# Stores of the residual and of finished gated blocks issued by GpSimd instead of ScalarE

## The chip, the cores and the metric

The kernel runs on one core of a Trainium2 chip. The metric is the device time of one execution in microseconds. Each time given for a kernel is the median of several runs. The profile comes from one more execution, recorded by the hardware profiler. In it PE is TensorE's matmuls, PEld its weight loads, DVE is VectorE, ACT is ScalarE, POOL is GpSimd and SP is SyncE. SP does no arithmetic here: it only issues transfers. A name with a q behind it (ACTq) is that engine's sequencer, which waits for semaphores and issues transfers while the engine itself works on.

## The reference, cut to what matters

One layer of an encoder over 1024 positions of width 1024, in float32. Two attentions share one input projection and one output projection; then comes a gated feed-forward block of width 2816. The part in which the change lies:

```python
h = h + jnp.einsum('bsd,df->bsf', mix, w_out)          # the residual h1
hn = rmsnorm(h, norm_ffn)
g = jnp.einsum('bsd,df->bsf', hn, w_gate)              # 1024 -> 2816
u = jnp.einsum('bsd,df->bsf', hn, w_up)
g = conv_width_3_over_positions(g) + conv_b
h = h + jnp.einsum('bsf,fd->bsd', silu(g) * u, w_down) # 2816 -> 1024
out = rmsnorm(h, norm_final)
```

## The kernel before

Everything is kept transposed: 128 features on the partitions, the 1024 positions along the free dimension, in two halves of 512. A float32 operand is split into a high and a low half, and each block product is three matmuls (high by high, high by low, low by high; function `group`, lines 986 to 988). The halves of the weights come from `split_w`: ACT copies the high half (line 960), DVE subtracts (line 961). In the attention the same is done at lines 169 and 170.

The stages in order of time, in the profiled execution: input projection and attention up to about 376 us, the output projection up to about 420 us, the gated block up to about 820 us, the down projection up to about 1016 us, and a tail in which the last columns are normed and stored.

**Output projection** (loop at line 1049). For each half h and each of 8 feature tiles d, PE makes a bank, and `settle_out` (line 1003) finishes the one before: DVE adds the residual input (line 1006), the sum h1 is stored to DRAM (`spilled`, line 1007), ACT squares it (line 1009) and DVE adds the squares up (line 1011). These are 16 stores of 256 KB. The sums in SBUF are later scaled in place for the norm (`normed`, line 1016) and turned into operands (`operand`, line 993), while the copies in DRAM are read back at the end (`residual`, line 1388) to be added to the down projection.

**Gated block** (class `Gated`). The products follow a scheme of seven instead of eight block products (names 11, 12, s1, s2, s4, s3, 22), so that sums and differences of operands and weights are made on DVE (`sub`, line 1025; lines 1095 to 1108). Each of 22 units makes gate and up for 128 features. `p1` and `p5` copy banks with ACT (`copy_bank`, line 1027), `p2`, `p3` and `p7` add with DVE (`join`, line 1026), `conv` does the convolution and SiLU (lines 1160 to 1163), and `p4` multiplies (lines 1170, 1171). Its result u, the finished gated block, is stored by `keep` (line 1188) to a tile `x` in DRAM. The first 11 units and the last 11 are paired; `sums` (line 1194) makes three differences of a pair (tiles t23 and t4) and stores them with `keep` too. That is 22 stores of a whole unit's block (512 KB), 11 of t23 (512 KB) and 11 of t4 (256 KB). For the first four units the store is put off: `to_keep` holds it, and the main loop does two at a time under `behind("joined")`, which queues it after the ACT evacuation marked "joined" (line 1151) on that evacuation's engine.

**Down projection** (loop at line 1452). It reads the stored blocks back (`x_load`, line 1303, issued by SP), splits them (`x_split`: ACT line 1309, DVE line 1310) and multiplies them with w_down, whose halves SP loads (`down_raw`, line 1277) four groups ahead. `x_load`, `down_raw` for all but the last product and `residual` keep their order on SP's queue. The feature tiles 2 and 5 are finished by POOL (line 1424), the others by DVE.

**What sets the order.** PE's order is the order of the program (it is scheduled by hand). The other engines' queues are laid out by a planner when the kernel is built. It goes by priorities and modelled times of all instructions, issues of transfers among them, and it assigns buffers too: tiles of one tag share a number of buffers (`op` 14, `mix` 8, `tt` 6), and a tile that takes a buffer over waits until the last reader of the former tile is done, a store included. Each queue then runs strictly in order. Before the change ACT issues the 60 stores, SP issues all loads, and POOL issues no transfer at all.

Of the kernel before, what the change touches and what calls it, by code (L numbers as in the profile page):

```python
# [56 lines left out]
def hybrid_layer(tc, xT, w_first, w_in, w_out, w_gate, w_up, w_down, small, sink, rpb, consts, rope, out):  # L57
    nc = tc.nc
    with ExitStack() as ctx:
# [13 lines left out]
        def big(name, tag, dt=F32):  # L73
            return lpool.tile([128, S], dt, name=name, tag=tag, bufs=slots[tag])
# [8 lines left out]
        tsl = lambda h: slice(h * HALF, (h + 1) * HALF)  # L83
# [20 lines left out]
        for name, dst, n in (("h", his, 2), ("h", his, 2), ("l", los, 2), ("l", los, 2), ("w", None, 2)):  # L104
            t = flat(big(name, "mix", F32R)[:, :], n)
# [581 lines left out]
        t = quarters(big("f", "mix"))  # L687
# [137 lines left out]
        for g in range(2):  # L825
            for b in range(NB):
                q, t = unit_window(g, b)
# [53 lines left out]
        for u in range(len(flat)):  # L881
            q, t, need, kind = flat[u]
# [69 lines left out]
        spilled = [dram.tile([128, S], F32, name="h1d", tag=f"h1d{d}") for d in range(KT)]  # L952
# [48 lines left out]
        at = lambda k, h: h1[k][:, tsl(h)]  # L1001

        def settle_out():
            d, h, ps = late.pop(0)
            with tc.high_priority(offset=500):
                nc.vector.tensor_tensor(sv(at(d, h)), pv(ps[:, :]), sv(at(d, h)), op=ALU.add)
            nc.scalar.dma_start(spilled[d][:, tsl(h)], at(d, h))
            s2 = half("s2")
            nc.scalar.activation(s2, at(d, h), AF.Square)
            if total[h] is not None:  # L1010
                nc.vector.tensor_tensor(s2, s2, total[h], op=ALU.add)
            total[h] = s2
# [36 lines left out]
        for h in range(2):  # L1049
            for d in range(KT):  # L1050
                if h == 0 and d + 2 < KT:
                    wo.append(load_wo(d + 2, fpool))
                ps = bank("pj", ("o", "s", "pj")[(h * KT + d) % 3])
                for _ in product(ps, wo[d], mg[4:8], h):
                    pass
                late.append((d, h, ps))
                if h == 1 and d == 1:
                    v = inverse_narrow([total[0]], D, "pt")
                settle_out()
                if h == 0 and d in (3, 4):  # L1060
                    pure((0, FT // 2)[d - 3])
                if h == 0 and d >= 5 or h == 1 and d == 0:
                    head_weights((d - 5) % KT, "s1")
                if h == 1 and d == 2:
                    wide = widen(v, "pt")
                    normed(0, wide, K1)
                    B[1, 1] = [operand(at(k, 0), "xg") for k in K1]
                if h == 1 and d == 4:
                    normed(0, wide, K2)
                    B[2, 1] = [operand(at(k, 0), "xg") for k in K2]  # L1070
# [48 lines left out]
        class Gated:  # L1119
# [48 lines left out]
            def p4(self):  # L1168
                ps, u = self.take("x", 0, "22", "t4", False), self.c
                join(u[:, 0:HALF], ps, self.cv[:, 0:HALF], ALU.mult)  # L1170
                nc.vector.tensor_tensor(u[:, HALF:S], u[:, HALF:S], self.cv[:, HALF:S], op=ALU.mult)
                k = self.f % FH
                if self.f < FH:
                    first_of[k] = u
                    sub(u[:, HALF:S], u[:, HALF:S], u[:, 0:HALF])
                    names = ("11", k), ("t1", k)
                else:
                    names = ("21", k), ("22", k)
                if self.f in FO[:HEAD]:
                    to_keep.append(lambda: keep(u, *names))  # L1180
                else:
                    keep(u, *names)
# [4 lines left out]

        def keep(t, *names):
            d = dram.tile([128, HALF * len(names)], F32, name="x", tag="x" + "_".join(f"{n}{k}" for n, k in names))
            nc.scalar.dma_start(d, t)  # L1190
            for i, name in enumerate(names):
                X[name] = d[:, i * HALF:(i + 1) * HALF]

        def sums(unit):
            k = unit.f % FH
            a, b = first_of.pop(k), unit.c
            t = big("t23", "mix")
            sub(t[:, 0:HALF], b[:, HALF:S], a[:, HALF:S])
            sub(t[:, HALF:S], t[:, 0:HALF], a[:, 0:HALF])
            keep(t, ("t2", k), ("t3", k))  # L1200
            t4 = half("t4")
            sub(t4, b[:, 0:HALF], t[:, 0:HALF])
            keep(t4, ("t4", k))
# [400 lines left out]
```

## Time and profile before

| | before |
|---|---|
| median of 3 runs | 1030.71 us (1030.1 to 1031.3) |
| the profiled execution | 1030.93 us |
| its span, first to last instruction | 1029.1 us |
| TensorE's granted clock over it | 0.998 |
| stores concerned | 60: 16 of 256 KB (line 1007), 33 of 512 KB and 11 of 256 KB (line 1190) |

Two transfer queues carry everything: the row q1 is that of SP and q10 that of ACT. The number of packets, the megabytes and the share of the time of the 16 DMA engines:

```profile
q1 hardware_dynamic: 57920, 118.69, 36.1%
q10 hardware_dynamic: 10224, 25.30, 6.3%
```

How to read the rows: a row of a timeline gives the start in us, the duration in us, the engine, the line of the kernel, the operation, the tile written and the tiles read with their shapes, how many instructions are merged in the row, and in brackets how long the engine stood idle before and for whom. A row of waits gives who waited for whom, the sum in us, how often, and the longest. A row of a group gives its count, its busy time, the mean duration of one in ns, and the idle time before.

### The profile page before, as it was taken

Reading aid. Unit: us, or ns where it says so; the run is one execution under the profiler, and the core shown is the slowest. Engines: PE = TensorE matmul, PEld = TensorE weight load, DVE = VectorE, ACT = ScalarE, POOL = GpSimd, SP = SyncE. Lnnn points to the kernel's source line nnn. Section 1 sums busy time; section 2 is a strip of 40 time slices with the busy share of each in tenths; the row PEclk is TensorE's granted clock in tenths of the full one; section 3 lists DMA queues with packets and bytes.
Section 4 is the critical chain, followed back from the end, with each engine's and each line's share of the span. In section 5 each row is a group of like instructions: output and inputs, shape, how many; then the busy total and the mean of one; then the engine's idle time right before and its main releaser. Section 6 shows DMA issues by size and latency. Waiting matters only on the chain.

```text
span 1029.1 us, 14858 instructions
## 1 busy us (share of the span) xinstructions
PE 1011.5 (98%) x5094; PEld 889.2 (86%) x5094; DVE 837.2 (81%) x1566; ACT 561.3 (55%) x1077; POOL 108.0 (10%) x188
## 2 busy tenths in 40 slices
PE   9999999999999999999999999999999999999997
PEld 8888888888888888888888888888888888888886
DVE  7889888768888799999988877786887877996675
ACT  8457776657676544555535444443444654554451
POOL 0133333232242100000000000000000000000002
PEclk9999999999999999999999999999999999999999
DMA  7222122333225247313353332333323788876644
GB/s 291 76 77 75 50 72 62 82 82 82 83 61 175 74 163 254 113 42 122 133 205 103 110 117 101 113 113 113 103 93 113 267 298 294 305 240 233 215 161 164
DMA packets 68220, 144.94 MB, mean 141 GB/s; under 512 B 8240, under 2 KB 18736, under 8 KB 68144
## 3 DMA queue, kind: packets, MB, share of 16 engines
q1 hardware_dynamic: 57920, 118.69, 36.1%
q10 hardware_dynamic: 10224, 25.30, 6.3%
q8 instruction: 40, 0.66, 0.3%
q14 instruction: 36, 0.29, 0.1%
HBM read 103.58 MB, written 28.57 MB: 128 GB/s over the span
## 4 chain that ended last, share of the span: by engine, by line
PE 74%; DVE 13%; ACT 7%; issue 3%; DMA 3%; POOL 0%; DVEq 0%; SPq 0%; ACTq 0%; POOLq 0%
PE dn L986 6%; PE dn L987 6%; PE dn L988 6%; PE x L986 6%; PE x L987 6%; PE x L988 6%; PE pj L177 5%; PE pj L178 5%; PE pj L179 5%; PE y L986 3%; PE y L988 3%; PE y L987 3%; PE s L389 2%; DVE pl L427 2%; ACT p L416 2%
## 5 line engine op out<-in xcount | busy, mean ns | idle before, releaser
L986 PE MATMUL x<-hg,whi 128*128 128x512 f32 x352 | 133.7, 380 | 1.7 <-ACT c L1027 1.4
L987 PE MATMUL x<-hg,whi 128*128 128x512 f32 x352 | 133.4, 379 | 0.0
L988 PE MATMUL x<-hg,wlo 128*128 128x512 f32 x352 | 133.4, 379 | 0.0
L986 PE MATMUL dn<-xd,whi 128*128 128x512 f32 (+1 forms) x330 | 120.8, 366 | 0.0
L987 PE MATMUL dn<-xd,whi 128*128 128x512 f32 (+1 forms) x330 | 120.5, 365 | 0.0
L988 PE MATMUL dn<-xd,wlo 128*128 128x512 f32 (+1 forms) x330 | 120.5, 365 | 0.0
L416 ACT ACTIVATE p<-p,nm 128x385 f32<-128x385 f32 (+3 forms) x128 | 74.9, 586 | 54.3 <-DVE nm L412 50.8
L177 PE MATMUL pj<-xgh,whi 128*128 128x512 f32 x245 | 99.8, 407 | 0.3 <-DVE v L339 0.3
L420 POOL TENSOR_SCALAR p<-p,sm 128x384 f32<-128x384 f32 (+1 forms) x128 | 78.8, 628 | 199.1 <-DVE sm L418 159.6
L960 ACT ACTIVATE whi<-ws 128x512 fp32r<-128x512 f32 (+1 forms) x100 | 60.6, 620 | 70.7 <-DVE ws L1099 15.0
L178 PE MATMUL pj<-xgl,whi 128*128 128x512 f32 x245 | 92.9, 379 | 0.0
L179 PE MATMUL pj<-xgh,wlo 128*128 128x512 f32 x245 | 92.9, 379 | 0.0
L960 ACT ACTIVATE whi<-raw 128x512 fp32r<-128x512 f32 (+1 forms) x102 | 60.7, 610 | 42.8 <-PE x L987 17.0
L961 DVE TENSOR_TENSOR wlo<-ws,whi 128x512 fp32r<-128x512 f32 (+1 forms) x100 | 66.6, 681 | 18.0 <-ACT whi L960 17.9
L427 DVE TENSOR_TENSOR pl<-pt,ph 128x384 fp32r<-128x384 f32 (+2 forms) x108 | 63.4, 589 | 20.4 <-ACT ph L426 18.3
L1309 ACT ACTIVATE xd<-xd 128x512 fp32r<-128x512 f32 x77 | 47.5, 626 | 55.1 <-DMA xd<-x 54.4
L986 PEld LDWEIGHTS x<-hg,whi 128*128 128x128 f32 x352 | 66.5, 189 | 11.9 <-ACT c L1027 1.8
L1424 POOL TENSOR_TENSOR h<-h,wide 128x256 f32<-128x256 f32 (+1 forms) x6 | 5.4, 915 | 672.8 <-ACT wide L1420 672.8
L1310 DVE TENSOR_TENSOR xd<-xd 128x512 fp32r<-128x512 f32 x77 | 52.4, 688 | 28.4 <-ACT xd L1309 28.1
L988 PEld LDWEIGHTS x<-hg,wlo 128*128 128x128 f32 x352 | 66.5, 189 | 9.5
L987 PEld LDWEIGHTS x<-hg,whi 128*128 128x128 f32 x352 | 66.5, 189 | 9.4
L988 PEld LDWEIGHTS dn<-xd,wlo 128*128 128x128 f32 x330 | 62.5, 189 | 7.7
(268 smaller groups left out, 2534.3 us busy)
## 6 DMA issues: line engine op xcount, KB each, us to landing
xd<-x SPq DMA_DIRECT2D x77, 256.0 KB, 5.0
raw<-in_w_down_dram SPq DMA_DIRECT2D x72, 256.0 KB, 4.4
raw<-in_w_gate_dram SPq DMA_DIRECT2D x22, 512.0 KB, 3.4
raw<-in_w_up_dram SPq DMA_DIRECT2D x22, 512.0 KB, 3.3
x<-c ACTq DMA_DIRECT2D x22, 512.0 KB, 2.6
raw<-in_w_in_dram SPq DMA_DIRECT2D x30, 256.0 KB, 2.9
raw<-in_w_down_dram SPq DMA_DIRECT2D x36, 192.0 KB, 4.5
x<-t ACTq DMA_DIRECT2D x11, 512.0 KB, 3.3
```

Source lines behind the costliest of these rows:

```text
L177: nc.tensor.matmul(ps, w[0], mv(x[0][:, tsl(h)]), start=first, stop=False)
L178: nc.tensor.matmul(ps, w[0], mv(x[1][:, tsl(h)]), start=False, stop=False)
L179: nc.tensor.matmul(ps, w[1], mv(x[0][:, tsl(h)]), start=False, stop=last)
L416: nc.scalar.activation(p[:, j, 0:e], p[:, j, 0:e], AF.Exp, bias=nm, scale=-1.0, accum_out=sm[:, j:j + 1])
L420: nc.gpsimd.tensor_scalar(p[:, i, 0:m], p[:, i, 0:m], sm[:, i:i + 1], 1.0, op0=ALU.mult, op1=ALU.mult)
L427: mark["rest"] = nc.vector.tensor_tensor(pl[:, 0:n], ps[:, 0:n], f32(ph[:, 0:n]), op=ALU.subtract)
L960: nc.scalar.activation(hi, src, AF.Copy)
L961: nc.vector.tensor_tensor(lo, src, f32(hi[:, :, :]), op=ALU.subtract)
L986: nc.tensor.matmul(ps, w[0], x[0], start=first and i == 0, stop=False, skip_group_check=True)
L987: nc.tensor.matmul(ps, w[0], x[1], start=False, stop=False, skip_group_check=True)
L988: nc.tensor.matmul(ps, w[1], x[0], start=False, stop=last and i == len(ws) - 1, skip_group_check=True)
L1310: nc.vector.tensor_tensor(lo, f32(lo), f32(hi), op=ALU.subtract)
```

## The change

Two stores change the engine that issues them; nothing else does.

```diff
             with tc.high_priority(offset=500):
                 nc.vector.tensor_tensor(sv(at(d, h)), pv(ps[:, :]), sv(at(d, h)), op=ALU.add)
-            nc.scalar.dma_start(spilled[d][:, tsl(h)], at(d, h))
+            nc.gpsimd.dma_start(spilled[d][:, tsl(h)], at(d, h))
             s2 = half("s2")
...
         def keep(t, *names):
             d = dram.tile([128, HALF * len(names)], F32, name="x", tag="x" + "_".join(f"{n}{k}" for n, k in names))
-            nc.scalar.dma_start(d, t)
+            nc.gpsimd.dma_start(d, t)
             for i, name in enumerate(names):
                 X[name] = d[:, i * HALF:(i + 1) * HALF]
```

All 60 stores pass from ACT's queue to POOL's. What they read and write, their sizes and what they wait for stay the same. For the four stores that are put off, `behind("joined")` names an instruction of ACT, and the stores are now on another queue.

## The prediction

> **What bounds the kernel now.** I read the engine totals first, to see which engine is full, then a table by stretches, cut where the work changes (output projection, opening of the gated stage, its steady part, down projection), then the waits of the tensor engine in the stretches from which stores are issued, and last the queues around each of these waits.
>
> ```profile
> span 1029.1 us, 14858 instructions
> ...
> PE 1011.5 (98%) x5094; PEld 889.2 (86%) x5094; DVE 837.2 (81%) x1566; ACT 561.3 (55%) x1077; POOL 108.0 (10%) x188
> ```
> ```profile
> 376.00:427.00 51.00, 50.32 (x240) 43.74 (x239) 47.33 (x78) 27.09 (x47) 0.00 (x0) 1.00 0.66 223
> 427.00:497.00 70.00, 68.59 (x321) 59.74 (x319) 69.12 (x108) 41.72 (x66) 0.00 (x0) 1.00 0.24 81
> 497.00:800.00 303.00, 303.00 (x1404) 265.35 (x1405) 238.22 (x345) 132.35 (x201) 0.00 (x0) 1.00 0.34 119
> 800.00:1016.00 216.00, 215.70 (x1052) 189.95 (x1051) 164.76 (x274) 108.40 (x190) 2.53 (x2) 1.00 0.73 249
> ```
>
> The columns of the second are the stretch and its length, then busy time (and instructions) of PE, PEld, DVE, ACT and POOL, the granted clock, the DMA share and GB/s. The profiled execution took 1030.93 us, of which 1029.1 are the span. PE is busy in all 303.00 us from 497 to 800 and in 215.70 of the next 216.00, at full clock, with 0.215 us from one matmul to the next. Nothing that ACT is spared shortens that. ACT is busy for 132.35 of the 303, so it has room for its issues there. PE is idle for 0.68 us in the first stretch, 1.41 in the second and 0.30 in the last. These are the waits behind that:
>
> ```profile
> PE x L986 <- ACT c L1027: 1.4, 1, 1.4
> PE sw L240 <- DVE v L233: 0.7, 1, 0.7
> ...
> PE x L986 <- ACT gs L1027: 0.3, 1, 0.3
> ```
>
> So the whole sum that could be won after 376 us, short of the tail, is 1.4 + 0.7 + 0.3 = 2.4 us. What counts as a change here is 0.2% of the median of 1030.71, which is 2.06 us, about what a measurement of this kernel can tell. From 376 to 497 the second column to watch is DVE: 47.33 of 51 and 69.12 of 70. There the two engines run level, and the chain of work that ended last runs through DVE:
>
> ```profile
> 449.35 4.82 DVE h L1025 x8
> 454.17 1.33 DVE ws L1025 x3
> ```
>
> **What the issues cost ACT, and what of it reaches PE.**
>
> ```profile
> L1190 ACTq DMA_DIRECT2D x<-c x22: 326/326/1132, 499.8 to 827.7; - x22
> L1190 ACTq DMA_DIRECT2D x<-t x22: 326/326/782, 501.2 to 830.6; - x22
> ...
> DMA to landing us min/median/max: 2.6/2.6/4.5
> ```
> ```profile
> L1007 ACTq DMA_DIRECT2D h1d<-h x16: 326/326/346, 377.1 to 418.1; - x16
> ...
> DMA to landing us min/median/max: 2.0/2.3/6.3
> ```
>
> The change takes 22 + 22 + 16 = 60 issues off ACT, at a median of 0.326 us: 60 x 0.326 = 19.6 us of its sequencer. It saves PE only what stands ahead of an evacuation that PE waits for. The 1.4 us wait is this piece of ACT's queue:
>
> ```profile
> 492.71 1.15 ACT L960 ACTIVATE whi<-ws 128x512 fp32r<-128x512 f32 x2 [1.34 <-DVE ws L1103]
> ...
> 494.29 1.05 ACT L1163 ACTIVATE cv<-cv 128x1024 f32<-128x1024 f32 x1
> 495.24 1.13 ACT L960 ACTIVATE whi<-raw 128x512 fp32r<-128x512 f32 x2
> 496.27 0.57 ACT L1027 ACTIVATE c<-x 128x512 f32<-128x512 f32 x1
> 499.80 0.33 ACTq L1190 DMA_DIRECT2D x<-c  x1
> ```
>
> The copy that PE wants (496.27) stands behind weight halves and a SiLU, and the first gated store is issued 3.5 us after it. Nothing is won. The 0.7 us wait is for a reciprocal in DVE's queue: nothing again. The 0.3 us wait is the one with a store in it:
>
> ```profile
> 809.52 0.63 ACT L1309 ACTIVATE xd<-xd 128x512 fp32r<-128x512 f32 x1
> 809.84 0.33 ACTq L1190 DMA_DIRECT2D x<-c  x1
> 810.21 0.60 ACT L1027 ACTIVATE gs<-x 128x512 f32<-128x512 f32 x1
> ```
>
> Without the issue the copy could begin when the activation before it ends, at 809.52 + 0.63 = 810.15: 0.06 us earlier. If the planner also puts the copy first, all 0.3 goes. I take 0.06.
>
> **The stores on POOL.** POOL does no work between the attention and the final scaling:
>
> ```profile
> 1005.67 2.53 POOL L1424 TENSOR_TENSOR h<-h,wide 128x512 f32<-128x512 f32 x2 [658.66 <-ACT wide L1420]
> ```
>
> It is idle for 658.66 us up to 1005.67, that is from 347 on, and the stores go from 377.1 to 830.9. Each waits in POOL's queue for DVE's last write. Only the next store stands behind it, and the scaling at 1005.67 long after. So the waits and the issues cost nothing there.
>
> No store of this kernel is issued by POOL, so its time to land is bounded. Below: ACT's 2.6 us. Above: the longest landing of such a store, 6.3, and on top one POOL instruction for making the transfer, as long as the longest kind that POOL runs here:
>
> ```profile
> L420 POOL TENSOR_SCALAR p<-p,sm 128x384 f32<-128x384 f32 (+1 forms) x128 | 78.8, 628 | 199.1 <-DVE sm L418 159.6 <-PE pt L526 11.8 <-PE pt L452 9.5
> L490 POOL TENSOR_TENSOR xb<-cst,rr 128x384 f32<-128x384 f32 x8 | 9.4, 1170 | 31.0 <-DMA rr<-in_rpb_dram 26.6 <-DVE nm L412 4.4
> ```
>
> 6.3 + 1.2 = 7.5 us; I take 2.6 + 1.2 = 3.8, since most landings lie at the median. Who waits for a landing? Buffers that are filled anew, and loads that read the store back:
>
> ```profile
> 397.20 0.33 ACTq L1007 DMA_DIRECT2D h1d<-h  x1
> 415.57 0.74 DVE L1016 SCALAR_TENSOR_TENSOR h<-h,par,sw 128x512 f32<-128x512 f32 x1
> 510.15 0.60 ACT L1027 ACTIVATE c<-x 128x512 f32<-128x512 f32 x1 [2.63 <-PE x L988]
> ```
>
> The residual issued at 397.20 is overwritten by L1016 at 415.57, 18.4 us later. By the order of the buffers, the gated block issued at 499.80 frees the one that the copy at 510.15 fills, 10.3 us later, and that copy waited for PE. Both leave over 2.8 us at the upper bound. The read-backs are the tight place: twice SP stands until a store has landed, and its later loads stand with it.
>
> ```profile
> SPq L1303 <- DMA x<-c: 10.0, 2, 5.1
> ```
> ```profile
> 819.78 1.39 DVE L961 TENSOR_TENSOR wlo<-raw,whi 128x512 fp32r<-128x512 f32 x2 [0.36 <-ACT whi L960]
> 829.09 0.38 PE L986 MATMUL dn<-xd,whi 128*128 128x512 f32 x1
> ```
>
> The store of 809.84 comes just before the first of the two. The weights made soonest before their use after it are the low halves ending at 819.78 + 0.69 = 820.47, for a group that starts at 829.09. That is 8.6 us of cover against 7.5 - 2.6 = 4.9 us of lateness at the upper bound: nothing. Without the cover it would cost PE the whole 1.2 to 4.9 us.
>
> **The four early blocks.** The stores of the first four gated blocks are kept back behind an evacuation on ACT's queue (499.80 and after). On POOL that place in the queue is not there, so they go when DVE has finished the blocks, some 10 us sooner, beside weight loads:
>
> ```profile
> 492.68 0.33 SPq L966 DMA_DIRECT2D raw<-in_w_up_dram  x1
> 501.67 0.68 DVE L1095 TENSOR_TENSOR ws<-raw 128x512 f32<-128x512 f32 x1
> raw<-in_w_up_dram SPq DMA_DIRECT2D x22, 512.0 KB, 3.3
> ```
>
> This load lands after about 3.3 us, at 496.0, and is used at 501.67: 5.7 us of cover. One store of the same size in its way costs at most its own 2.6 us, two 5.2. Hidden; uncovered, it would be those 2.6 to 5.2.
>
> **POOL beside DVE.** This is the one unknown with a price. The same DVE instruction, two operands in SBUF, during the attention, where POOL works on SBUF 95.58 of 304.00 us by the table of stretches:
>
> ```profile
> 56.00:360.00 304.00, 298.39 (x1697) 264.13 (x1697) 250.80 (x657) 208.07 (x512) 95.58 (x165) 1.00 0.30 81
> L170 DVE TENSOR_TENSOR wlo<-raw,whi 128x512 fp32r<-128x512 f32 x34 | 25.9, 763 | 2.6 <-ACT whi L169 2.3
> L170 DVE TENSOR_TENSOR wlo<-raw,whi x38: 670/685/1258, 29.2 to 356.9; 128x512 fp32r<-128x512 f32 x38
> ```
>
> Its median is 685 ns, its mean there 763, its longest 1258. So POOL's work makes DVE wait: (763 - 685) / (95.58 / 304.00) = 0.25 us for each meeting, 0.57 at most. Up to 20 stores (16 residuals, 4 early blocks) would fall between 376 and 497, where DVE has no room: from 0 to 20 x 0.57 = 11.5 us, with 20 x 0.25 = 5.0 in between. I take 0, because a store does no arithmetic on a tile in SBUF as those POOL instructions do, and keep the rest as a rival.
>
> The Trainium skill bears on this in its page "SBUF — State Buffer", section "Who interferes with whom". A VectorE instruction with two SBUF inputs contends with a GpSimd instruction that reads SBUF, but not with one that only writes it; a GpSimd-issued transfer has its descriptors written by GpSimd. By that rule the term is 0; read as any work on POOL delaying such an instruction, it is 5.0. The rows above agree with the first half of the rule, and no run here yet shows the second.
>
> **The sum.** 1030.93 - 0.06 = 1030.87 us for an execution like the profiled one, which lay 0.22 above the median. For the median that is 1030.65, so 1030.7: no change.
>
> **The rivals.**
> 1. *DVE is held up by POOL* (slower). Between 376 and 497 each store delays the DVE instruction that runs beside it. For it: L170's 763 against 685, and DVE busy for 69.12 of 70. Against it: the delayed cases are beside POOL arithmetic. Price 5.0 us: 1035.7; at most 11.5: 1042.2. It decides from 2.06 / 20 = 0.10 us for each store.
> 2. *The planner lays the queues out worse* (slower). The order of ACT and DVE is planned from modelled times, and after 376 us it may shift when ACT's issues go. One evacuation more behind a SiLU costs 1.4 us as at 496.27, two 2.8: 1033.5. Against it: from 497 to 800 ACT is under half busy.
> 3. *The planner lays them out better* (faster). All three waits go: 1030.7 - 2.4 = 1028.3. It needs nearly all of them to pass 2.06 us.
> 4. *POOL's stores land far later than my bound*, or the end of the program waits for POOL. Past 2.6 + 8.6 = 11.2 us PE waits for weights; outside the span there are 1.83 us now, and as much again gives 1032.5.
>
> **How the numbers follow.** No change 0.47; rival 1 0.20; rival 2 0.17; rival 3 0.12; rival 4 0.04. The slower ones are 0.41 together. The forecast's own range is 1029.2 to 1032.2. The range given is 1028.5 to 1037.0: below it lies about half of rival 3, above it the upper part of rival 1 and some of rival 4, some 0.14 together. The chances are 0.12 for faster, 0.47 for within 0.2% and 0.41 for slower.
>
> **What would show it.** Right: 60 store issues on POOL's queue and none on ACT's; PE at 303.0 from 497 to 800; DVE's two-operand instructions still at 685 ns from 376 to 497; landings under 7.5 us; the 1.4 us wait still there. Rival 1: such instructions of 0.8 us and more beside a store, and a later end of the DVE chain. Rivals 2 and 3: another order in ACT's queue near 496 and 810, and other waits of PE. The forecast is wrong if PE's waits after 376 us sum to over 4.5 us, or to under 0.4.

## The result, and the profile after

| | before | after |
|---|---|---|
| median of 6 runs | 1030.41 us (1029.72 to 1031.30) | 1037.79 us (1035.64 to 1039.86) |
| the profiled execution | 1030.93 us | 1035.64 us |
| its span | 1029.1 us | 1033.9 us |

The ratio is 1.0068, with a 95% interval of 1.0057 to 1.0078: the changed kernel is slower by 0.7%, some 7.4 us. The profiled execution is the lowest of its six, so it shows only 4.7 us of the loss; a second profile, further down, shows the rest.

The same table of stretches as before the change, now of the changed kernel:

```profile
376.00:427.00 51.00, 47.55 (x224) 41.12 (x223) 45.71 (x75) 26.30 (x45) 8.88 (x16) 1.00 0.64 220
427.00:497.00 70.00, 70.00 (x330) 61.31 (x329) 68.00 (x106) 39.41 (x62) 1.07 (x2) 1.00 0.28 93
497.00:800.00 303.00, 301.60 (x1398) 263.79 (x1397) 240.73 (x348) 136.50 (x206) 20.38 (x38) 1.00 0.33 117
800.00:1016.00 216.00, 215.50 (x1036) 189.35 (x1036) 165.37 (x274) 108.51 (x190) 4.68 (x6) 1.00 0.74 249
```

PE, the first number behind the comma, now misses 3.45 of the first 51 us, where it missed 0.68. The 1.40 us missing from 497 to 800 are the wait that stood at 496.9 before; it has slid past the border of the stretch. The waits of PE in the changed kernel, with the sum, the count and the longest:

```profile
PE sw L240 <- DVE v L233: 3.8, 2, 3.1
PE x L986 <- ACT c L1027: 1.4, 1, 1.4
...
PE x L986 <- ACT gs L1027: 0.5, 1, 0.5
PE ss L221 <- DVE s L1011: 0.3, 1, 0.3
```

Most of what is new is one wait. PE transposes the reciprocal of line 233 to scale the first half of the residual, and the wait for it has grown from 0.7 to 3.1 us. To see why, the order of DVE's queue just before that reciprocal has to be read in both kernels. DVE before the change:

```profile
400.69 0.68 DVE L1006 TENSOR_TENSOR h<-pj,h 128x512 f32<-128x512 f32 x1
401.29 0.68 DVE L223 TENSOR_REDUCE v<-ss 128x4 f32<-128x512 f32 x1
401.89 0.68 DVE L961 TENSOR_TENSOR wlo<-ws,whi 128x512 fp32r<-128x512 f32 x1
402.49 0.68 DVE L961 TENSOR_TENSOR wlo<-raw,whi 128x512 fp32r<-128x512 f32 x1
403.09 0.17 DVE L233 RECIPROCAL v<-v 128x4 f32<-128x4 f32 x1
```

And after it:

```profile
400.66 0.68 DVE L1006 TENSOR_TENSOR h<-pj,h 128x512 f32<-128x512 f32 x1
401.26 0.68 DVE L1035 TENSOR_TENSOR ws<-raw 128x512 f32<-128x512 f32 x1
402.64 0.69 DVE L961 TENSOR_TENSOR wlo<-ws,whi 128x512 fp32r<-128x512 f32 x1 [0.70 <-ACT whi L960]
403.25 0.68 DVE L961 TENSOR_TENSOR wlo<-raw,whi 128x512 fp32r<-128x512 f32 x1
403.85 0.68 DVE L1006 TENSOR_TENSOR h<-pj,h 128x512 f32<-128x512 f32 x1
404.45 0.68 DVE L223 TENSOR_REDUCE v<-ss 128x4 f32<-128x512 f32 x1
405.74 0.69 DVE L1025 TENSOR_TENSOR ws<-ws,raw 128x512 f32<-128x512 f32 x1 [0.61 <-DMA raw<-in_w_gate_dram]
406.35 0.17 DVE L233 RECIPROCAL v<-v 128x4 f32<-128x4 f32 x1
```

The same instructions stand in another order. The reduction (line 223) began at 401.29 and now begins at 404.45, behind a weight addition, two weight subtractions, of which one waits 0.70 us for ACT, and another residual addition. Then a subtraction for the weights s2 (line 1025) has come between it and the reciprocal, and that one waits 0.61 us for its load. No line of DVE's work was touched by the change. It is the planner's layout that moved. It changed only for DVE and ACT, from the output projection on (213 of the 573 places on DVE and 85 of the 346 on ACT); PE's order, SP's order and the rest of POOL's are the same in both programs.

How long each stage took, from the starts of four instructions of PE (the first matmul of the output projection, the first into a gated bank, the first and the last of the down projection) and the end of the span. The first row begins at about 313 us, because part of the output projection is already done between pieces of the attention:

| us | before | after | after, second profile |
|---|---|---|---|
| output projection | 103.51 | 106.53 | 109.76 |
| gated block | 401.98 | 402.17 | 402.02 |
| down projection | 201.45 | 201.44 | 201.44 |
| from its last matmul to the end | 8.97 | 10.23 | 9.79 |

The stages between lose 0.2 us or nothing. The loss is the output projection (3.02 us in one profile, 6.25 in the other) and the tail (1.26 and 0.82); 0.24 and 0.09 us come from ahead of these stages.

POOL itself does what was foreseen. Its stores of the changed kernel, with the minimum, median and maximum of an issue in ns, and one line for the landing:

```profile
L1190 POOL DMA_DIRECT2D x<-c x22: 531/532/547, 490.6 to 832.7; - x22
L1190 POOL DMA_DIRECT2D x<-t x22: 531/542/553, 504.8 to 835.5; - x22
```
```profile
L1007 POOL DMA_DIRECT2D h1d<-h x16: 539/539/757, 377.6 to 421.8; - x16
...
DMA to landing us min/median/max: 2.2/3.5/5.1
```

### The profile page after: what moved, and what is told of

Same layout as the page of the kernel before. It is cut to its first block, busy times and chain, and to the rows that moved or that the text cites. A ratio compares the mean times of both kernels' runs of the same rounds, so it can differ in the third digit from the quotient of the medians.

```text
span 1033.9 us, 14912 instructions
## 1 busy us (share of the span) xinstructions
PE 1012.5 (98%) x5094; PEld 889.8 (86%) x5094; DVE 838.4 (81%) x1566; ACT 562.8 (54%) x1077; POOL 140.1 (14%) x248
## 4 chain that ended last, share of the span: by engine, by line
PE 74%; DVE 13%; ACT 5%; DMA 4%; issue 2%; POOL 0%; DVEq 0%; SPq 0%; ACTq 0%; POOLq 0%
PE dn L986 6%; PE dn L987 6%; PE dn L988 6%; PE x L986 6%; PE x L988 6%; PE x L987 6%; PE pj L177 5%; PE pj L178 5%; PE pj L179 5%; PE s L389 3%; PE y L987 3%; PE y L988 3%; PE y L986 3%; DVE wlo L961 2%; PE z L988 2%
## 5 line engine op out<-in xcount | busy, mean ns | idle before, releaser
L961 DVE TENSOR_TENSOR wlo<-raw,whi 128x512 fp32r<-128x512 f32 (+1 forms) x102 | 66.6, 668 | 4.5 <-ACT whi L960 4.5
L987 PEld LDWEIGHTS dn<-xd,whi 128*128 128x128 f32 x330 | 62.5, 189 | 7.7
```

Source lines behind the costliest of these rows:

```text
L961: nc.vector.tensor_tensor(lo, src, f32(hi[:, :, :]), op=ALU.subtract)
L987: nc.tensor.matmul(ps, w[0], x[1], start=False, stop=False, skip_group_check=True)
```

## The experiments

Two theories were set against each other. The *plan theory*: moving the stores changed the order in which DVE's and ACT's work was laid out, and that order is the loss. The *store theory*: a store costs more when POOL issues it. In rows of the experiments the line numbers are larger by up to 7, since lines were added to the kernels. Ratios are to the kernel before, run on the same chip.

**One half of the change at a time.** In the first, line 1190 goes back to ACT, in the second line 1007:

```diff
 def keep(t, *names):
-            nc.gpsimd.dma_start(d, t)
+            nc.scalar.dma_start(d, t)
```

> Only the 16 residual stores (line 1007) go to POOL; the 44 gated stores stay on ACT. Plan theory (DVE's queue is laid out differently in the output projection, and the reciprocal of line 233 stands behind a weight subtraction that waits for a load): most of the loss of 7.4 us is here, PE waits 3.3 us or more for that reciprocal, so 1033.7 to 1036.7 us. Store theory (what a store costs when POOL issues it, wherever): 16 of 60 stores carry 16/60 x 7.4 = 2.0 us, so 1032.4, with no long wait for the reciprocal.

> Only the 44 gated stores (line 1190) go to POOL; the 16 residual stores stay on ACT. Plan theory: the wait for the reciprocal near 403 us is back at 0.7 us as before, and only the longer tail of 1.4 us is left, so 1030.4 to 1031.8 us. Store theory: 44/60 x 7.4 = 5.4 us are left, so 1035.8.

Measured: residual stores alone 1036.50 us, ratio 1.0050 (1.0037 to 1.0063); gated stores alone 1031.53 us, ratio 1.0007 (0.9998 to 1.0016). So the 16 residual stores alone lose 5.4 us on that chip, most of the loss, and the 44 gated ones 0.4 us, which the interval does not tell from nothing. The kernel with the 16 alone has the changed kernel's order of DVE up to the reciprocal, and its wait:

```profile
PE sw L240 <- DVE v L233: 4.2, 2, 3.5
```

The other has 1.6 us in that row, in two waits, the longer of 1.0. Its order of DVE differs from the one before as well, but only from 505 us on: a new order is not a loss in itself.

**The order without the move, and the move without the order.** To each kernel an ordering edge was added between every two neighbours on DVE's and on ACT's queue, from the output projection on; the stores were left free.

```diff
         hybrid_layer(tc, *args)
+        known = {i.name: i for i in nc.cur_bb.bb.instructions}
+        for queue in QUEUES:
+            for p, q in zip(queue, queue[1:]):
+                tc.add_manual_dep(known[f"I-{q}"], f"I-{p}", mybir.DependencyInfo(
+                    mybir.DependencyClass.NoSync, mybir.DependencyReason.DATA), reason="order")
```

> All 60 stores on POOL, but from the output projection on the compute instructions of DVE and ACT are held in the order that they had before the change. Plan theory: PE's waits are those of before (0.7, 1.4, 0.3 us), the tail alone may cost 1.4 us, so 1030.4 to 1031.8. Store theory (POOL's issues, landings or what they do to DVE): the order matters nothing, so 1037.8.

> All 60 stores stay on ACT, but DVE and ACT are held in the order that the changed kernel has. Plan theory: PE waits 3.3 us or more for the reciprocal near 403 us though no store is on POOL, so 1033.7 to 1036.7 us. Store theory: 1030.4.

Measured: all stores on POOL in the order of before, 1031.24 us, ratio 1.0002 (0.9993 to 1.0011). All stores on ACT in the order of after, 1037.78 us, ratio 1.0065 (1.0052 to 1.0078). In the profiles, DVE and ACT do run in the order that was asked for (but for one instruction in the second, behind 800 us). This decides it: the order without the move costs 6.7 us, and the move without the order changes the whole time by nothing that can be measured. The waits of PE with the stores on POOL and the order of before:

```profile
PE x L992 <- ACT c L1033: 1.4, 1, 1.4
PE sw L246 <- DVE v L239: 0.6, 1, 0.6
PE ss L234 <- ACT s L1448: 0.6, 1, 0.6
```

The gap at the reciprocal is 0.2 us here (the 0.6 is the wait in the tail), and the 0.3 us wait for `gs` near 810 is gone. What these give the tail takes back: 10.03 us in place of 8.97.

A gap is counted here and below from 0.215 us after the start of the last matmul ahead of it, when the next could have started. The profile shows that last one busy for some 0.16 us more, so a gap is that much longer than the wait in PE's rows: 0.84 us before the change, where the wait is 0.68.

The kernel with the order alone missed its range on the upper side, by 1.1 us. PE's wait for the reciprocal was 3.5 us, as expected; there was another of 1.4 us just ahead of it, for the sum of squares (line 1011 of the kernel before). Its table of stretches, cut at that wait, shows what had not been counted:

```profile
404.00:407.69 3.69, 0.18 (x1) 0.00 (x0) 2.99 (x7) 0.97 (x3) 0.00 (x0) 1.00 0.70 243
407.69:409.10 1.41, 1.41 (x9) 1.30 (x10) 1.41 (x3) 0.00 (x0) 0.00 (x0) 0.99 0.02 6
409.10:412.50 3.40, 3.40 (x10) 2.68 (x9) 2.23 (x4) 1.67 (x3) 0.00 (x0) 0.50 0.68 206
412.50:415.90 3.40, 3.40 (x17) 2.99 (x16) 3.24 (x6) 1.68 (x3) 0.00 (x0) 1.00 0.27 102
```

The granted clock (third number from the end) falls to 0.50 for 3.4 us after the wait. PE is busy there, but does 10 matmuls where the next 3.40 us hold 17. Half of 3.4 us, 1.7 us, is lost on top of the wait. The kernel with the residual stores alone has the same piece from 407.60 to 411.00. The profiled execution of the changed kernel does not: its gap of 3.30 us stayed at full clock.

```profile
403.27:406.57 3.30, 0.17 (x1) 0.00 (x0) 2.69 (x7) 0.84 (x2) 0.54 (x1) 1.00 0.87 290
406.57:410.00 3.43, 3.42 (x18) 3.08 (x19) 3.43 (x6) 1.58 (x3) 0.54 (x1) 1.00 0.36 118
```

**Which part of the order.** Two small edits of the changed kernel. The first queues the subtractions behind the reciprocal; the second, besides, puts the reduction ahead of the last weight addition.

```diff
+                mark["inverse"] = nc.vector.reciprocal(v[:, 0:n], v[:, 0:n])
...
+                    mark["first"] = mark["inverse"]
...
             u.p5()
-            head_weights(i, "s2")
+            with behind("first"):
+                head_weights(i, "s2")
```
```diff
+                    tc.add_manual_dep(mark["added"].ins, mark["reduce"].ins.name, mybir.DependencyInfo(
+                        mybir.DependencyClass.NoSync, mybir.DependencyReason.DATA), reason="order")
```

> All 60 stores on POOL; only the subtractions of line 1025 that make the weights s2 are queued behind the reciprocal of line 233. Load theory (the reciprocal is late because such a subtraction waits for its load ahead of it): the reciprocal comes about 0.9 to 1.5 us sooner, PE's wait falls from 3.3 to 3.7 us to about 2.3, the clock is not cut, so 1032 to 1033 us. Rival (the order before that, a reduction that starts 3.2 us late, is all of it): nothing changes, 1036 to 1038.

> As the run that holds the subtraction, and besides the addition of line 1035 for the fourth head unit is queued behind the reduction of line 223, which then runs when its operand is there. If these two places are the whole loss, PE waits 0.2 to 1.2 us as before the change: 1030.4 to 1031.5 us. If other changes of the order cost time too: 1033 or more.

Measured: 1036.49 us, ratio 1.0048 (1.0036 to 1.0060), and 1032.49 us, ratio 1.0014 (1.0006 to 1.0023). The first is in the range of the rival, so my load theory fell; the second lies between its two ranges. The longest wait for the reciprocal (last number), with the first edit and then with both:

```profile
PE sw L240 <- DVE v L233: 3.1, 3, 2.2
```
```profile
PE sw L240 <- DVE v L233: 1.1, 2, 0.6
```

In the one profile of the first edit PE's gap did shrink to 2.4 us, at full clock, but that execution took 1034.42 us, and the other four took 1036.28 to 1037.07. The late reduction is the larger part: with both edits the gap is 0.6 us (the 0.6 in the row is the wait in the tail). 1.4 us over before are left, and the profile has most of it at the end: 10.25 us from the last matmul of the down projection, 1.28 more than before, while the sum of PE's gaps is 0.3 us more. So the two places are nearly all of the loss of the output projection, and not that of the tail. The edits changed 18 and 32 of the 1566 places on DVE in all, more than the ones named, so this is less clean than the runs with a held order.

**The wait alone, made longer.** Stores on ACT and the order of before, with the reduction repeated:

```diff
-                    nc.vector.tensor_reduce(v, ps[:, 0:n * 128].rearrange("p (c w) -> p c w", w=128), axis=mybir.AxisListType.X, op=ALU.add)
+                    for _ in range(1 + again):
+                        nc.vector.tensor_reduce(v, ps[:, 0:n * 128].rearrange("p (c w) -> p c w", w=128), axis=mybir.AxisListType.X, op=ALU.add)
```

> Stores on ACT and the order of before; the reduction ahead of the reciprocal is done four times in place of once, which lengthens PE's wait of 0.8 us by 3 x 0.6 = 1.8 us, to 2.6 us. Both theories: 1.8 us over before, 1032.9 us where before takes 1031.1, at full clock.

> The same with the reduction done seven times: PE's wait becomes 0.8 + 6 x 0.6 = 4.4 us. Wait-only theory: 3.6 us over before, 1034.7 us. Clock theory (past some 3.4 us of idleness PE runs at half clock for 3.4 us, which costs 1.7 us more): 5.3 us over before, 1036.4 us, and the granted clock is 0.5 for some 3.4 us behind the wait.

Measured: 1035.04 us (1032.08 to 1036.94), ratio 1.0036 (1.0023 to 1.0049), and 1037.01 us (1035.83 to 1037.60), ratio 1.0053 (1.0040 to 1.0066). The wait-only theory's 1034.7 for the seven reductions is excluded by every run. Four reductions cost more than both theories said. The profile shows why: on that execution a weight load came 1.43 us late for DVE,

```profile
398.72 0.69 DVE L1042 TENSOR_TENSOR ws<-raw 128x512 f32<-128x512 f32 x1 [1.43 <-DMA raw<-in_w_up_dram]
```

so that the gap was 3.38 us and not 2.6, and the clock was cut. The stretches around the gap, first with four reductions, then with seven:

```profile
403.15:406.53 3.38, 0.17 (x2) 0.00 (x1) 3.31 (x7) 0.82 (x2) 0.00 (x0) 1.00 0.82 266
...
407.20:410.60 3.40, 3.40 (x9) 2.65 (x9) 3.03 (x5) 2.23 (x4) 0.00 (x0) 0.50 0.20 77
```
```profile
402.80:407.36 4.56, 0.14 (x2) 0.01 (x1) 4.42 (x9) 0.82 (x2) 0.00 (x0) 0.76 0.46 156
407.36:412.00 4.64, 4.64 (x13) 3.92 (x14) 3.78 (x6) 2.33 (x4) 0.00 (x0) 0.50 0.15 57
```

The longer gap is followed by 4.64 us at half clock, worth 2.3 us.

**A second profile of the changed kernel.**

> The changed kernel once more, for a second profile. Clock theory: a run above 1037 us has the granted clock at 0.5 for 3.4 us or more behind the wait near 407 us, and one of about 1035.7 has not. Wait-only theory: the clock is full there in every run and a slower run has a longer wait instead, of 5 us and more.

Measured: 1038.21 us (1037.04 to 1038.87), ratio 1.0065 (1.0052 to 1.0077); the profiled execution is the median. It answers for the clock theory, and in part for the other: the wait is longer as well.

```profile
404.20 0.68 DVE L223 TENSOR_REDUCE v<-ss 128x4 f32<-128x512 f32 x1
406.19 0.69 DVE L1025 TENSOR_TENSOR ws<-ws,raw 128x512 f32<-128x512 f32 x1 [1.30 <-DMA raw<-in_w_gate_dram]
406.80 0.17 DVE L233 RECIPROCAL v<-v 128x4 f32<-128x4 f32 x1
```
```profile
403.00:407.00 4.00, 0.20 (x1) 0.00 (x0) 2.70 (x7) 0.84 (x2) 0.54 (x1) 0.82 0.77 280
407.00:412.40 5.40, 5.38 (x15) 4.47 (x16) 3.66 (x6) 1.86 (x3) 0.54 (x1) 0.50 0.41 146
412.40:416.00 3.60, 3.60 (x19) 3.15 (x18) 3.07 (x5) 1.90 (x3) 0.54 (x1) 1.00 0.18 73
```

The load came 0.69 us later than in the first profile (1.30 against 0.61 us of waiting), the gap became 3.99 us, and then PE ran for 5.40 us at half clock, which loses 2.70. The gap is 3.15 us longer than the 0.84 of before. 3.15 + 2.70 = 5.85 of the 6.25 us that the output projection lost. With the tail's 0.82 that is nearly all of the 7.2 us between the two spans (1036.3 and 1029.1).

**The old order with two instructions moved.** The copy of line 1027 for which PE waited 1.4 us goes up by three places, and the reciprocal by one. All else is the order of before.

> Stores on ACT, DVE and ACT in the order of before with two instructions moved: the copy of line 1027 that PE waits 1.4 us for near 497 us goes ahead of a SiLU and two weight halves, and the reciprocal of line 233 near 403 us goes ahead of one weight subtraction. If these waits are worth what the gaps show, 1.5 us and up to 0.6 us go: 1029.0 us where before takes 1031.05. If they only move elsewhere (the weights behind are late instead): 1030.5 to 1031.5.

> The same order with all 60 stores on POOL. The gaps go as in the run with the stores on ACT, the 0.3 us wait near 810 us goes too, and the tail is 0.8 us longer: 1029.5 us. If a store on POOL costs something elsewhere: 1031 or more.

Measured: with the stores on ACT 1029.80 us, ratio 0.9991 (0.9982 to 1.0000); with the stores on POOL 1029.97 us, ratio 0.9990 (0.9981 to 0.9999). Both lie between the two expectations. The gap at the reciprocal went in both; the other shrank only from 1.57 to 0.89 us. So the kernel with the stores on POOL and this order is 0.1% under the kernel before. Its interval just leaves out 1, but 0.1% is half of what the prediction counts as a change. It is 0.8% under the changed kernel as it ran on the same chip (1038.21 us).

## Why the prediction was wrong

**The step that failed** is the one on the waits: "The 0.7 us wait is for a reciprocal in DVE's queue: nothing again." I asked of each wait only what a store on ACT added to it, with the queues as they stood, and set the forecast on that, 0.06 us. But the reciprocal's place is laid out from all modelled times, and it had no slack, since PE already waited for it: it is the end of a chain through DVE, ACT and DVE (reduction, root, reciprocal) that PE waits for, on a DVE with 47.33 of 51 us busy. My own views held both facts, the wait and the full DVE. The runs showed in place of "nothing" a gap longer by 2.46 us in one profile and 3.15 in the other. Why the planner chose so is argued only, and no run shows it: without the stores, ACT's squares and halves come earlier in its model, and DVE's weight work then counts as ready ahead of the reduction.

**Rival 2** named the cause, the planner's layout, at 0.17. It was mis-sized and misplaced. I priced it in ACT's queue, at two evacuations behind a SiLU (2.8 us), and held against it a stretch, 497 to 800, that has nothing to do with it. It came at DVE, at 403 us: 3.15 us of gap in the median run. To this I added nothing for the clock, which cost nothing in the first profile of the changed kernel and 2.7 us in the second, and nothing for the tail. With the terms of the second profile the rival's price would have been 3.15 + 2.70 + 0.82 = 6.7 us and the time 1037.4; 1037.79 was measured. That sum is put together afterwards and forecasts nothing.

**POOL costs nothing beside DVE: right.** Rival 1 is out. In the changed kernel, from 376 to 500 us, the mean of a two-operand instruction is what it was (685 ns):

```profile
L961 DVE TENSOR_TENSOR wlo<-raw,whi 128x512 fp32r<-128x512 f32 x15 | 10.0, 684 | 1.6 <-ACT whi L960 1.6
```

By the rule quoted from the Trainium skill ("SBUF — State Buffer", "Who interferes with whom") the term is 0. The trace agrees with its second half too, for stores issued by GpSimd: 684 ns beside them. A mean could hide a few late ones, but the 65 additions and subtractions of this size on DVE that overlap an issue of POOL in that profile, from 370 us on, took 679 to 693 ns.

**Issues and landings on POOL: right.** An issue takes 0.53 to 0.54 us there, not 0.33, on an engine that has nothing else to do. (My bound took line 490 for POOL's longest kind of instruction; line 1424 has one of 1.29 us, which makes it 7.6 us and changes nothing.) The 16 residual stores land in at most 5.1 us, below the bound, and no wait of PE stems from the landing of a store. All 60 on POOL with the old order come out at a ratio of 1.0002.

**The four early blocks: hidden, as said.** The first gated store goes at 490.6 where it went at 499.8, and the gated block takes 0.2 us more or less.

**Rival 4, the end waits for POOL: right in kind, small.** Line 1599 holds SP's closing waits, before and after:

```profile
L1599 SPq EVENT_SEMAPHORE  x7: 17/28/410, 1026.8 to 1029.1; - x7
```
```profile
L1599 SPq EVENT_SEMAPHORE  x11: 17/28/28, 1030.1 to 1033.8; - x11
```

There are four more. In all five profiles with no store on POOL the span ends 8.9 to 9.0 us after the start of the last matmul of the down projection; with the residual stores there, 9.3; with the gated ones or all, 9.8 to 10.3. The traces let this be taken apart at the end of PE's last instruction. From there to the end of the span it is 5.7 to 5.9 us with no store on POOL, 6.2 with the residual ones, and 6.6 to 6.7 with the gated ones or all, whichever order is held: some 0.8 us come with the move. Ahead of that point it is 3.1 us in ten of the thirteen profiles. In the other three (the changed kernel's first, the run that holds the order of before, the one with both small edits) PE's clock drops before its last transposes are done, and it is 3.4 to 3.6.

**The tests that I had set.** PE's waits after 376 us and ahead of the tail sum to 3.1 + 1.4 + 0.5 + 0.3 = 5.3 us, above the 4.5 at which the forecast was to count as wrong. "The 1.4 us wait still there" held, which shows that this test could not tell the cases apart.

## What to carry to other kernels

Where a planner lays out the queues, an edit on one engine can be an edit on the others: price it by the chains with the least slack ahead of PE, wherever they lie, and not only at the instructions that it touches. To tell a change's own cost from that of the new layout, hold the old order and make the change, and hold the new order and leave the change out; two runs settle it. If the order is what was tuned, hold it before trying anything else. Pinning two places, a reduction and a reciprocal, left 1.4 us of the loss here; holding the whole order left 0.1.

## What the runs showed of the hardware

A gap of PE can have a second price, and it comes in steps of 3.41 us. The traces record when the granted clock was 0.50; around 405 us that was:

| profile | gap, us | clock at 0.50, us | for, us |
|---|---|---|---|
| changed kernel, first | 3.30 | never | 0 |
| four reductions | 3.38 | 407.16 to 410.57 | 3.41 |
| residual stores alone | 3.68 | 407.63 to 411.04 | 3.41 |
| the order alone | 3.68 | 409.06 to 412.48 | 3.41 |
| changed kernel, second | 3.99 | 405.56 to 412.39 | 6.83 |
| seven reductions | 4.59 | 405.16 to 411.99 | 6.83 |

The Trainium skill, page "TensorE: Matmul & The Clock Gate", section "HAM oscillation — how this bites in real kernels", gives as its rule that PE should have no idle gaps of more than about 3.4 us. The trace agrees in size, though half clock already followed a gap of 3.38 us, which is a wait of 3.21 us in PE's rows.

Length may not be what decides. Half clock does not begin with the gap's end: it begins 0.6 us after it with four reductions, 1.4 us after it with the order alone, and 1.5 us ahead of it in the second profile of the changed kernel. In each of the five profiles in which it comes here, it comes again in the tail, and that begins 621.23 or 624.64 us later, which is 182 or 183 times 3.4133 us. So in these five it begins on marks 3.41 us apart, and it can matter where the marks fall in a gap. If the same spacing is counted back from the half clock in the tail of the first profile of the changed kernel (1025.90 us), the marks lie at 401.26, 404.67 and 408.09 us: one of them divides the gap, and PE is idle for at most 1.90 us between two of them. Between the two marks ahead of half clock in the other five it is idle for 2.03 to 2.79 us. This is read from the traces only. No run moved a gap against the marks, and in the tail half clock also came after less than 1.90 us, so no threshold is shown.

For the changed kernel it means that a load which is 0.7 us late can move the time by over 2 us, as between its two profiles (1035.64 and 1038.21 us). Its six runs spread over 4.2 us and the six of before over 1.6, but 21 runs of before on another chip spread over 4.2 us as well, so the spread is no evidence of it.
